# A projection tile's two moving pieces meet at a token that depends on the tile's index

## The chip, the cores and the metric

The kernel runs on one core of a Trainium2 chip. The metric is the device time of one execution in microseconds (us). Before the change three runs took 1004.9, 1005.52 and 1005.81 us; the median is 1005.52 us. A core has a matrix engine (TensorE, PE in the profile, with a loader for its weights, PEld), a vector engine (VectorE, DVE), a scalar engine (ScalarE, ACT), GpSimd (POOL) and a queue engine that issues most of the transfers (SyncE, SP). They run side by side and meet through semaphores.

## The reference: what is computed

The kernel is one layer of a hybrid sequence model over L = 528 tokens: 16 learned meta tokens and then 512 real ones, each 2048 wide. After a root-mean-square norm one input projection gives all the quantities of two branches; the branches' outputs are joined, go through an output projection and are added to the residual, and a last norm follows.

```python
hn = _rmsnorm(h_res, norm_in_g[l])
P = hn @ w_in[l]
Pr, Pc = P[..., :RW_COLS], P[..., RW_COLS:]
prev = jnp.pad(Pr[:, :-1], ((0, 0), (1, 0), (0, 0)))
Pr = Pr + (prev - Pr) * mu_shift[l]          # r, k, v, g of 1024 columns, and two of 64
...
y = _rwkv7_recurrence(...)                   # 16 heads of 64, in chunks of 64 tokens
y_a = (yn + bonus) * jax.nn.silu(g_r)
y_b = Bg * _causal_depthwise_conv(Cg * hc, conv_w[l]) * jax.nn.silu(g_c)
mix = jnp.concatenate([y_a, y_b], axis=-1)
h_res = h_res + mix @ w_out[l]
out = _rmsnorm(h_res, norm_f_g)[:, N_META:]
```

The first branch needs, for each token, the token before it (the shift by `mu_shift`), the second a convolution over three tokens. The meta tokens are dropped at the end, but k and v of the meta tokens enter the recurrence.

## The kernel before

**The projection.** The product `hn @ w_in` is made of 65 output tiles of 128 columns each: eight each of r, k, v and g of the first branch, one called lora (the two 64-wide parts), and eight each of B, C, h and gc of the second branch. The results stand with the 128 columns on the partitions and the tokens along the free axis. Input and weights are each split into a high and a low part in a rounded 32-bit format (`xh`, `xl`; `hi`, `lo` of a weight tile `w`), and three products make up the result: hi by xh, hi by xl, lo by xh. The contraction of 2048 runs in 16 blocks of 128 (`kt`). Each matmul instruction loads a 128 x 128 block of weights (the stationary operand, an LDWEIGHTS in the profile) and streams token columns past it (the moving operand); its result goes to a bank of PSUM that holds 512 such columns.

**The pieces.** Since 528 or 514 tokens don't go into one bank, the tokens are cut into two pieces, each with a PSUM tile of its own. There are three sets of ranges. `FULL` (k, v, lora) is tokens 0 to 256 and 256 to 528. `TAIL` (r, C, h, g) leaves out the meta tokens but for the last two, which shift and convolution need: 14 to 272 and 272 to 528. `REAL` (B, gc) is tokens 16 to 528 in one piece. The generator `steps` issues, for a quarter of the contraction (four blocks), first the twelve matmuls of the first piece and then the twelve of the second: 48 matmuls per piece and 96 per tile of two pieces. The piece's tokens are read from `xh` and `xl`, which have a row of 576 32-bit words per block.

**After the matmuls.** `scaled` multiplies each piece by the tokens' norm factor on DVE, from PSUM into one SBUF tile (`pr` or another); `shift_full` and `shift_real` add the shift, with one operation on ACT and one or two on DVE.

**What sets the order.** TensorE's order is written out by hand. `mains` is a generator that issues the projection's matmuls one by one, in the order of `plan`, and yields for each the time that it is reckoned to take, 0.43 ns a column. The rest of the program (`prepare` for a pair of heads, `invert`, the recurrence) issues its own matmuls and calls `fill(ns)` in between, which takes steps of `mains` until their reckoned times add up to that many ns; so projection matmuls fill the time in which the chain of the recurrence waits for other engines. `later(ns, ...)` puts off a transfer in the same reckoned time. The other engines' order is set by a scheduler from the order of issue and priorities; transfers on SP follow in that order too. Weights come ahead of use: three buffers for the raw halves of a tile (`wr`), six for split quarters (`w`); ACT makes the high part (L138), DVE or POOL the low one (L139).

The lines that matter: `FULL` and `TAIL` at L313 to L315, the matmul at L326 in `steps`, `main`, `scaled` (L345), `shift_full` and `shift_real`, the uses in `use`, and the loop at the end of `mains`. The first four tiles (lora, k, r, B, all of index 0) are issued by `mains` itself with the constant ranges. Recurrence lines named below: L451 sums for the norm factor, L674 products of a pair's chunks, L999 and L1003 the recurrence's chunk step, L1236 the output projection.

Of the kernel before, what the change touches and what calls it, by code (L numbers as in the profile page):

```python
# [23 lines left out]
L = SEQ + META  # L24
# [57 lines left out]
def hymba_kernel(ctx: ExitStack, tc: tile.TileContext, xt, xtok, front, w_in, w_out, pv, lup, cst, msk, gf, out):  # L82
# [33 lines left out]
    tile_of = {"r": 0, "k": 8, "v": 16, "g": 24, "lora": 32, "B": 33, "C": 41, "h": 49, "gc": 57}  # L116
    for what, i in plan:
        m = tile_of[what] + i
# [58 lines left out]
    def tm(name):  # L177
        return tp.tile([P, LP], F32, tag="tm", name=name, bufs=3)
# [134 lines left out]
    FULL = ((0, 256), (256, L))  # L313
    TAIL = ((14, 272), (272, L))
    REAL = ((META, L),)  # L315

    def steps(ps, ranges, k4, q, ks=range(4), rs_=range(2)):
        hi, lo = quarters[q]
# [12 lines left out]
    def banks(ranges, name, pool, tag):  # L331
        return [pool.tile([P, b - a], F32, tag=tag, name=f"ps_{name}_{r}") for r, (a, b) in enumerate(ranges)]

    def main(j, ranges, name):
        prefetch(2 * j + 4)
        ps = banks(ranges, name, pm, "main")
        for k4 in range(4):
            if k4 == 1:
                prefetch(2 * j + 5)
            yield from steps(ps, ranges, k4, 4 * j + k4)  # L340
        return ps

    def scaled(ranges, ps, dst, base):
        for (a, b), p in zip(ranges, ps):
            nc.vector.tensor_tensor(out=dst[:, a - base : b - base], in0=p, in1=rs[:, a:b], op=ALU.mult)  # L345

    def shift_full(ps, m, name, dst):
        pr = tp.tile([P, L + 1], F32, tag="pr", name=f"pr_{name}", bufs=2)
        nc.gpsimd.memset(pr[:, 0:1], 0.0)
        scaled(FULL, ps, pr, -1)  # L350
        sh = tm(f"sh_{name}")[:, 0:L]
        nc.scalar.activation(sh, pr[:, 0:L], AF.Copy, scale=col(V_MU, m))
        for (a, b), d in dst:
            nc.vector.scalar_tensor_tensor(
                out=d, in0=pr[:, a + 1 : b + 1], scalar=omm[:, m : m + 1], in1=sh[:, a:b], op0=ALU.mult, op1=ALU.add
            )

    def shift_real(ps, m, name, dst):
        pr = tp.tile([P, L + 1], F32, tag="pr", name=f"pr_{name}", bufs=2)
        scaled(TAIL, ps, pr, 14)  # L360
        sh = tm(f"sh_{name}")[:, 0:SEQ]
        nc.scalar.activation(sh, pr[:, 1 : SEQ + 1], AF.Copy, scale=col(V_MU, m))
        nc.vector.scalar_tensor_tensor(
            out=dst, in0=pr[:, 2 : SEQ + 2], scalar=omm[:, m : m + 1], in1=sh, op0=ALU.mult, op1=ALU.add
        )

    def padded(t):
        return (((0, META), t[:, 0:META]), ((META, L), t[:, CH:LP]))
# [5 lines left out]

    def use_lora(ps):
        pre = tm("lora_pre")[:, 0:L]
        shift_full(ps, 32, "lora", (((0, L), pre),))
        th = tr("lora_th")[0:64, 0:L]
        al = tr("lora_al")[0:64, 0:L]
        nc.scalar.activation(th, pre[0:64], AF.Tanh)  # L380
        nc.vector.tensor_copy(al, pre[64:128])
        for j, t in enumerate((th, al)):
            nc.scalar.copy(la[0:64, j], t)
            nc.vector.tensor_tensor(out=la[64:128, j], in0=t, in1=la[0:64, j].bitcast(F32), op=ALU.subtract)
# [6 lines left out]
    def use(what, i, ps):  # L391
        if what == "lora":
            use_lora(ps)
        elif what in ("k", "v"):
            t = cq.tile([P, LP], F32, tag=what, name=f"{what}{i}")
            nc.gpsimd.memset(t[:, META:CH], 0.0)
            shift_full(ps, tile_of[what] + i, f"{what}{i}", padded(t))
            got[what, i] = t
        elif what in ("r", "g"):
            t = cq.tile([P, SEQ], F32, tag=f"r{i % 2}" if what == "r" else "g", name=f"{what}{i}")  # L400
            shift_real(ps, tile_of[what] + i, f"{what}{i}", t)
            if what == "g":
                gate(t, f"r{i}")
                later(14000, lambda: nc.sync.dma_start(gated[i], t))
            got[what, i] = t
        elif what == "C":
            u = tm(f"u{i}")
            scaled(TAIL, ps, u, 14)
            got[what, i] = u
        elif what == "h":  # L410
            u = got["C", i]
            hh = tm(f"hh{i}")
            with behind_of("turned"):
                scaled(TAIL, ps, hh, 14)
            n = SEQ + 2
            nc.gpsimd.tensor_tensor(out=u[:, 0:n], in0=u[:, 0:n], in1=hh[:, 0:n], op=ALU.mult)
            cv = tp.tile([P, SEQ], F32, tag="cw", name=f"cv{i}")
            nc.scalar.activation(cv, u[:, 0:SEQ], AF.Copy, scale=col(V_CW, i))
            for j in (1, 2):
                with behind_of("conv"):  # L420
                    nc.vector.scalar_tensor_tensor(
                        out=cv, in0=u[:, j : j + SEQ], scalar=col(V_CW, 8 * j + i), in1=cv, op0=ALU.mult, op1=ALU.add
                    )
            got[what, i] = cv
            if i == 0:
                nc.gpsimd.tensor_tensor(out=cv, in0=cv, in1=got["B", 0], op=ALU.mult)
        elif what == "B":
            b = tm(f"b{i}")[:, 0:SEQ] if i else tp.tile([P, SEQ], F32, name="b0")
            scaled(REAL, ps, b, META)
            got[what, i] = b  # L430
            if i:
                nc.gpsimd.tensor_tensor(out=got["h", i], in0=got["h", i], in1=b, op=ALU.mult)
        else:
            cv = got["h", i]
            g = tm(f"gc{i}")[:, 0:SEQ]
            with behind_of("split"):
                scaled(REAL, ps, g, META)
            gate(g, f"c{i}")
            o = direct.get(8 + i, cv)
            nc.vector.scalar_tensor_tensor(out=o, in0=cv, scalar=0.5, in1=g, op0=ALU.mult, op1=ALU.mult)  # L440
            if o is cv:
                later(9000, lambda: nc.sync.dma_start(mixd[8 + i], cv))
        ready.add((what, i))
# [29 lines left out]
    def mains():  # L473
        pa = banks(FULL, "lora", pm, "main")
        pb = banks(FULL, "k0", pz, "tz")
        pc = banks(TAIL, "r0", pm, "main")
        pd = [pi.tile([P, SEQ], F32, tag="ser", name="ps_B0")]
        four = ((pa, FULL), (pb, FULL), (pc, TAIL), (pd, REAL))
        for k in range(4):
            for n, (ps, rg) in enumerate(four):  # L480
                if k == n == 0:
                    hi, lo = quarters[0]
                    for ww, xx, first in ((hi, xh, True), (lo, xh, False), (hi, xl, False)):
                        for p, (a, b) in zip(ps, rg):
                            nc.tensor.matmul(p, ww[:, 0:P], xx[:, 0, a:b], start=first, stop=False)
                            yield (b - a) * 0.43
                    continue
                yield from steps(ps, rg, 0, 2 * n, (k,))
        for k4 in range(1, 4):
            for n, (ps, rg) in enumerate(four):  # L490
                h = 4 * (k4 // 2) + n
                if k4 == 2:
                    prefetch(h + 3)
                if (k4, n) == (3, 3):
                    for ks, part in ((range(1), 0), (range(1, 3), 4), (range(3, 4), None)):
                        yield from steps(ps, rg, k4, 2 * h + k4 % 2, ks)
                        if part is not None:
                            token_scale(yb, part)
                        if part == 4:
                            use("lora", 0, pa)  # L500
                            use("k", 0, pb)
                    continue
                for r in range(2 if n < 3 else 1):
                    if (k4, n, r) == (3, 1, 1):
                        yb = token_scale_sums()
                    yield from steps(ps, rg, k4, 2 * h + k4 % 2, range(4), (r,))
        use("r", 0, pc)
        use("B", 0, pd)
        for j in range(4, len(plan)):
            what, i = plan[j]  # L510
            rg = FULL if what in ("k", "v") else REAL if what in ("B", "gc") else TAIL
            ps = yield from main(j, rg, f"{what}{i}")
            if (what, i) == ("h", 0):
                state["conv"] = low[4 * j + 6]
            if what == "gc" and i < 4:
                state["split"] = low[4 * j + 4]
            use(what, i, ps)
# [1001 lines left out]
```

## Time and profile before

| What | Value |
|---|---|
| Median of three runs | 1005.52 us (1004.9 to 1005.81) |
| Span of the profiled execution, first to last instruction | 1003.4 us |
| Granted TensorE clock over the span | 0.998 |
| TensorE busy | 992.7 us, 9,723 matmuls |
| Weight loads busy | 914.6 us |
| DVE, ACT, POOL busy | 681.1, 394.9, 272.1 us |
| Mean transfer rate | 174 GB/s |

The profile is of one execution; only its span is told, so the 2.1 us between it and the median are taken as what lies around the span. A row of a group names the line, engine, operation, the tile written and those read, shapes and the count, then the time that its instructions cover and the mean length of one. A row of the timeline has the start in us from the span's start and the time covered, then engine, line, operation, tiles, shapes and how many neighbours were merged. A row of the chain has start, length, engine, tile, line and count. A row of a window has its bounds, its length, TensorE's busy time with the count, the granted clock, the transfers' share and rate. Matmuls overlap, so their lengths add up to more than the time they take; the distance from one start to the next is what a stream of them costs.

### The profile page before, as it was taken

What the parts mean: (1) busy time and instruction counts of PE and PEld (TensorE: products, weight loads), DVE (VectorE), ACT (ScalarE), POOL (GpSimd) and SP (SyncE); (2) the same over time, 40 slices, a digit from 0 to 9 for tenths busy, and PEclk for the clock granted to TensorE, in tenths of its full rate; (3) what the DMA queues carried; (4) which work ended last, traced back from release to release, by engine and by line L of the source; (5) the groups of instructions that cost most, each with busy time, mean ns of one, the idle gap of its engine ahead of it and who ended that gap; (6) DMA issues with size and microseconds to landing.
All of it is one profiled execution on the core that took longest, in us unless ns stands there. A gap on an engine that the chain in (4) does not pass through costs nothing.

```text
span 1003.4 us, 23673 instructions
## 1 busy us (share of the span) xinstructions
PE 992.7 (99%) x9723; PEld 914.6 (91%) x9723; DVE 681.1 (68%) x1247; ACT 394.9 (39%) x729; POOL 272.1 (27%) x284
## 2 busy tenths in 40 slices
PE   9999999999999999999999999999999999999996
PEld 8999999999998999998999998989889898788885
DVE  6777866587765569655569654245554597997897
ACT  7553423344323434323434322223232435546453
POOL 0122524233232323232423223223332333001001
PEclk9999999999999999999999999999999999999999
DMA  9525485546665364864263855968674688797654
GB/s 322 153 90 148 122 222 147 163 122 148 162 167 170 102 166 94 221 163 119 85 171 98 219 148 162 324 204 247 201 228 93 178 267 211 187 299 191 159 127 168
DMA packets 185036, 174.82 MB, mean 174 GB/s; under 512 B 121568, under 2 KB 142816, under 8 KB 184416
## 3 DMA queue, kind: packets, MB, share of 16 engines
q1 hardware_dynamic: 182336, 164.40, 57.0%
q0 software_dynamic: 2304, 8.39, 4.9%
q8 instruction: 76, 1.25, 0.5%
q10 hardware_dynamic: 288, 0.52, 0.1%
q14 instruction: 32, 0.26, 0.1%
HBM read 136.92 MB, written 36.35 MB: 173 GB/s over the span
## 4 chain that ended last, share of the span: by engine, by line
PE 91%; DVE 5%; issue 1%; DMA 1%; ACT 0%; POOL 0%; DVEq 0%; SPq 0%; ACTq 0%; POOLq 0%
PE ps_h L326 9%; PE ps_k L326 9%; PE ps_v L326 9%; PE ps_g L326 9%; PE ps_C L326 9%; PE ps_r L326 9%; PE ps_B L326 9%; PE ps_gc L326 9%; PE M L1236 5%; PE P L1236 2%; PE g L674 2%; DVE o L1207 2%; PE Q L1236 1%; PE ps_lora L326 1%; PE zs L999 1%
## 5 line engine op out<-in xcount | busy, mean ns | idle before, releaser
L139 POOL TENSOR_TENSOR w<-wr,w 128x512 fp32r<-128x512 f32 x119 | 172.2, 1447 | 360.9 <-ACT w L138 305.1
L138 ACT CAST w<-wr 128x512 fp32r<-128x512 f32 x252 | 153.2, 618 | 289.0 <-PE ps_C L326 48.7
L139 DVE TENSOR_TENSOR w<-wr,w 128x512 fp32r<-128x512 f32 x133 | 98.5, 746 | 104.4 <-ACT w L138 104.0
L326 PE MATMUL ps_k<-xh,w 128*128 128x256 f32 (+1 forms) x512 | 96.1, 285 | 0.0
L326 PE MATMUL ps_r<-xh,w 128*128 128x258 f32 (+1 forms) x512 | 95.1, 281 | 0.0
L326 PE MATMUL ps_v<-xh,w 128*128 128x272 f32 (+1 forms) x512 | 94.9, 284 | 0.0
L326 PE MATMUL ps_h<-xh,w 128*128 128x256 f32 (+1 forms) x512 | 94.6, 283 | 0.0
L326 PE MATMUL ps_C<-xh,w 128*128 128x256 f32 (+1 forms) x512 | 93.2, 281 | 0.0
L326 PE MATMUL ps_g<-xh,w 128*128 128x256 f32 (+1 forms) x512 | 92.1, 281 | 0.0
L326 PE MATMUL ps_B<-xh,w 128*128 128x512 f32 x256 | 83.5, 395 | 0.0
L326 PE MATMUL ps_gc<-xh,w 128*128 128x512 f32 x256 | 81.6, 393 | 0.0
L326 PEld LDWEIGHTS ps_k<-xh,w 128*128 128x128 f32 x512 | 80.4, 190 | 0.5
L326 PEld LDWEIGHTS ps_h<-xh,w 128*128 128x128 f32 x512 | 79.6, 188 | 1.3 <-issue 0.6
L326 PEld LDWEIGHTS ps_r<-xh,w 128*128 128x128 f32 x512 | 80.1, 188 | 0.3
L326 PEld LDWEIGHTS ps_v<-xh,w 128*128 128x128 f32 x512 | 79.9, 189 | 0.3
L326 PEld LDWEIGHTS ps_C<-xh,w 128*128 128x128 f32 x512 | 79.2, 188 | 0.6
L326 PEld LDWEIGHTS ps_g<-xh,w 128*128 128x128 f32 x512 | 79.1, 189 | 0.3
L326 PE MATMUL ps_k<-xl,w 128*128 128x256 f32 (+1 forms) x256 | 72.8, 284 | 0.0
L326 PE MATMUL ps_v<-xl,w 128*128 128x256 f32 (+1 forms) x256 | 72.6, 284 | 0.0
L326 PE MATMUL ps_h<-xl,w 128*128 128x258 f32 (+1 forms) x256 | 71.9, 281 | 0.5 <-issue 0.5
L326 PE MATMUL ps_g<-xl,w 128*128 128x258 f32 (+1 forms) x256 | 72.3, 282 | 0.0
L326 PE MATMUL ps_r<-xl,w 128*128 128x258 f32 (+1 forms) x256 | 72.0, 281 | 0.0
(321 smaller groups left out, 2258.9 us busy)
## 6 DMA issues: line engine op xcount, KB each, us to landing
wr<-in_w_in_dram SPq DMA_DIRECT2D x126, 512.0 KB
ct<-opd SPq DMA_DIRECT2D x64, 288.0 KB
wo<-in_w_out_dram SPq DMA_DIRECT2D x24, 512.0 KB
x<-in_w_out_dram POOLq DMA_DIRECT2D x16, 512.0 KB, 6.0
opd<-ar SPq DMA_DIRECT2D x8, 576.0 KB
opd<-gt SPq DMA_DIRECT2D x16, 288.0 KB
opd<-bt SPq DMA_DIRECT2D x64, 64.0 KB
x<-in_w_out_dram SPq DMA_DIRECT2D x8, 512.0 KB
```

Of the source, the lines that this page charges most:

```text
L138: nc.scalar.copy(hi, rq)
L139: low[q] = eng.tensor_tensor(out=lo, in0=rq, in1=hi.bitcast(F32), op=ALU.subtract).ins
L326: nc.tensor.matmul(ps[r], ww[:, w], xx[:, kt, a:b], start=(kt == 0 and n == 0), stop=(kt == KT - 1 and n == 2))
L674: nc.tensor.matmul(z[h][:, c - c0], bk[hs, c, h : h + 2, :].rearrange("p a s -> p (a s)"), ar[hs, c].rearrange("p a s -> p (a s)"), start= ...
L999: nc.tensor.matmul(d[hs, j], w, x[hs], start=(a == 0), stop=(a == b - 1))
L1207: last = nc.vector.tensor_tensor(out=lo, in0=rq, in1=hi.bitcast(F32), op=ALU.subtract)
L1236: nc.tensor.matmul(bank[s], left(prod, jj, m, s), w, start=(jj == 0 and n == 0), stop=(jj == 7 and n == 2))
```

## The change

The border between the two pieces becomes a function of the tile's index i (0 to 7), the same for k and v, and the same for r, C, h and g. lora keeps the old border, B and gc their single piece.

```diff
     FULL = ((0, 256), (256, L))
     TAIL = ((14, 272), (272, L))
     REAL = ((META, L),)
+    FULL_AT = (256, 264, 272, 260, 288, 264, 258, 280)
+    TAIL_AT = (272, 270, 274, 276, 286, 270, 280, 272)
+
+    def pieces(what, i):
+        if what in ("B", "gc"):
+            return REAL
+        if what in ("k", "v"):
+            return (0, FULL_AT[i]), (FULL_AT[i], L)
+        return (14, TAIL_AT[i]), (TAIL_AT[i], L)
...
-    def shift_full(ps, m, name, dst):
+    def shift_full(ps, m, name, dst, rg):
...
-        scaled(FULL, ps, pr, -1)
+        scaled(rg, ps, pr, -1)
...
-    def shift_real(ps, m, name, dst):
+    def shift_real(ps, m, name, dst, rg):
...
-        scaled(TAIL, ps, pr, 14)
+        scaled(rg, ps, pr, 14)
...
-            scaled(TAIL, ps, u, 14)
+            scaled(pieces(what, i), ps, u, 14)
...
-            rg = FULL if what in ("k", "v") else REAL if what in ("B", "gc") else TAIL
-            ps = yield from main(j, rg, f"{what}{i}")
+            ps = yield from main(j, pieces(what, i), f"{what}{i}")
```

With L = 528 the pieces of index 0 to 7 have these columns, first and second: for k and v 256 and 272, 264 and 264, 272 and 256, 260 and 268, 288 and 240, 264 and 264, 258 and 270, 280 and 248; for r, C, h and g 258 and 256, 256 and 258, 260 and 254, 262 and 252, 272 and 242, 256 and 258, 266 and 248, 258 and 256.

More of the change, by code (lines that the diff above doesn't have):

```diff
@@ L376, in use_lora @@
         pre = tm("lora_pre")[:, 0:L]
-        shift_full(ps, 32, "lora", (((0, L), pre),))
+        shift_full(ps, 32, "lora", (((0, L), pre),), FULL)
         th = tr("lora_th")[0:64, 0:L]
@@ L396, in use @@
             nc.gpsimd.memset(t[:, META:CH], 0.0)
-            shift_full(ps, tile_of[what] + i, f"{what}{i}", padded(t))
+            shift_full(ps, tile_of[what] + i, f"{what}{i}", padded(t), pieces(what, i))
             got[what, i] = t
@@ L400, in use @@
             t = cq.tile([P, SEQ], F32, tag=f"r{i % 2}" if what == "r" else "g", name=f"{what}{i}")
-            shift_real(ps, tile_of[what] + i, f"{what}{i}", t)
+            shift_real(ps, tile_of[what] + i, f"{what}{i}", t, pieces(what, i))
             if what == "g":
@@ L413, in use @@
             with behind_of("turned"):
-                scaled(TAIL, ps, hh, 14)
+                scaled(pieces(what, i), ps, hh, 14)
             n = SEQ + 2
```

## The prediction

> **What bounds the kernel now.** I read the page's head and the clock row first, then the chain of waits, then two long windows, then the waits of the weight loader, and last the timeline inside single projection tiles.
>
> ```profile
> span 1003.4 us, 23673 instructions
> PE 992.7 (99%) x9723; PEld 914.6 (91%) x9723; DVE 681.1 (68%) x1247; ACT 394.9 (39%) x729; POOL 272.1 (27%) x284
> PEclk9999999999999999999999999999999999999999
> PE 91%; DVE 5%; issue 1%; DMA 1%; ACT 0%; POOL 0%; DVEq 0%; SPq 0%; ACTq 0%; POOLq 0%
> ```
> ```profile
> 55.00:605.00 550.00, 549.98 (x5219) 1.00 0.57 147
> 605.00:845.00 240.00, 239.53 (x3464) 1.00 0.72 216
> ```
> ```profile
> PEld ps_B L326 <- DVE w L139: 0.4, 1, 0.4
> ```
>
> TensorE is busy for 99% of the span at a full clock, and it makes up 91% of the chain that ended last. The windows leave it 0.02 us idle in 550 us and 0.47 us in the next 240 us. The only wait of a projection tile for split weights in the whole trace is 0.4 us. So between 55 and 845 us time is matmuls laid end to end, and what counts is how far apart two of them start. The listed duration of a matmul (some 280 ns) overlaps with its neighbours and is of no use for that.
>
> The start-to-start spacing can be read off the timeline: take two starts of the xl matmuls of one piece; between neighbouring xl matmuls lie three spacings.
>
> ```profile
> 469.83 0.28 PE L326 MATMUL ps_k<-xl,w 128*128 128x256 f32 x1
> ...
> 470.89 0.28 PE L326 MATMUL ps_k<-xl,w 128*128 128x256 f32 x1
> ...
> 471.25 0.28 PE L326 MATMUL ps_k<-xl,w 128*128 128x272 f32 x1
> ...
> 472.36 0.29 PE L326 MATMUL ps_k<-xl,w 128*128 128x272 f32 x1
> ```
> ```profile
> 132.26 0.28 PE L326 MATMUL ps_C<-xl,w 128*128 128x258 f32 x1
> ...
> 133.34 0.28 PE L326 MATMUL ps_C<-xl,w 128*128 128x258 f32 x1
> ...
> 133.69 0.28 PE L326 MATMUL ps_C<-xl,w 128*128 128x256 f32 x1
> ...
> 134.71 0.28 PE L326 MATMUL ps_C<-xl,w 128*128 128x256 f32 x1
> ```
> ```profile
> 620.71 0.28 PE L326 MATMUL ps_C<-xl,w 128*128 128x256 f32 x1
> ...
> 621.77 0.28 PE L326 MATMUL ps_C<-xl,w 128*128 128x256 f32 x1
> ```
> ```profile
> 132.30 11.20 PE ps_C L326 x96
> 469.87 11.57 PE ps_k L326 x96
> 532.78 11.54 PE ps_v L326 x96
> 619.32 11.38 PE ps_C L326 x96
> 819.75 10.90 PE ps_B L326 x48
> ```
>
> Each pair of rows spans nine spacings. A full tile (k): 1.06/9 = 117.8 ns at 256 columns from token 0, 1.11/9 = 123.3 ns at 272 columns from token 256. A tail tile (C): 1.08/9 = 120.0 ns at 258 columns from token 14, and 256 columns from token 272 take 113.3 ns in the first C tile and 117.8 ns in a later one. The same shape thus has two speeds, 4.5 ns apart, which is also the difference between the chain's 11.20 and 11.38 us for a C tile. A 512-column matmul takes 10.90/48 = 227.1 ns.
>
> **The change part by part.** It alters no product and no count: TensorE still issues 9,723 matmuls and as many weight loads. It moves the border between the two pieces in 38 tiles: k and v with index 1 to 7 (14 tiles), r, C, h and g with index 1 to 6 (24 tiles); each piece has 48 matmuls. Index 0, index 7 of the tail tiles, lora, and the one-piece tiles B and gc stay. Were time strictly in proportion to columns, the border would not matter, since a tile keeps its 528 or 514 columns. Three things can break that.
>
> First, pieces under 256 columns. The full tiles get 240 (index 4) and 248 (index 7), the tail tiles 254, 252, 242 and 248 (index 2, 3, 4, 6). That is 2 + 16 + 2 = 20 pieces, 960 matmuls. No row shows a matmul of this kind with fewer than 256 columns. What a matmul costs when there is almost nothing to stream is seen elsewhere:
>
> ```profile
> 45.10 0.81 PE L451 MATMUL pss<-cs,accd 128*128 128x1 f32 x6
> L451 PE MATMUL pss<-cs,accd 128*128 128x1 f32 x8 | 0.9, 240 | 0.0
> ```
> ```profile
> L999 PEld LDWEIGHTS zs<-ct 64*64 64x64 f32 x256 | 13.1, 136 | 0.0
> L326 PEld LDWEIGHTS ps_k<-xl,w 128*128 128x128 f32 x256 | 48.3, 189 | 0.2
> ```
>
> Six matmuls of one column, each with its own 128-column weights, take 0.81 us with the last one's 0.25 us: (0.81 - 0.25)/5 = 112 ns apart. They wait for their weights: a load of 64 columns lasts 136 ns and one of 128 lasts 189, so 53 ns per 64 columns, some 106 ns for 128. Every projection matmul has such a load too. So below 256 columns I expect a floor instead of a gain: at least 112 ns, at most the 117.8 ns of 256 columns. I take 115.5, the mean of the two speeds of the nearest row, 256 columns from token 272.
>
> On TensorE: Matmul & The Clock Gate of the Trainium skill (section Back-to-back issue gap) speaks against this floor with its isolated gap, N/2.4 + 2.5 ns, linear in N; by it a 240-column matmul would take an estimated 102.5 ns and every border would cost the same, so that the change would be worth nothing (first rival). The same page's LDWEIGHTS section gives P/1.2, 107 ns for 128 columns, and there the trace agrees (106 ns).
>
> Second, the wider partner. From 256 to 272 columns I interpolate 117.8 to 123.3 (0.344 ns a column), above that 123.3 to 227.1 at 512 (0.43 ns a column): 280 columns 126.8, 288 columns 130.2.
>
> Third, where a piece begins. On that line 258 columns would be 118.5 ns; the tail's first piece, which begins at token 14 (byte 56, off a multiple of 16), takes 120.0. I charge 1.5 ns for every piece that begins at a token not a multiple of 4: the new borders 258, 270, 274 and 286. From below this may be nothing (the two extra columns explain it).
>
> Now each pair against today's. Full tiles, 117.8 + 123.3 = 241.1 ns; indices 1 to 7: 264+264 0.0; 272+256 (115.5 at an even border) -2.3; 260+268 0.0; 288+240 130.2 + 115.5 = +4.6; 264+264 0.0; 258+270 +1.5; 280+248 +1.2. Sum +5.0 ns, x 48 x 2 kinds = +0.5 us. Tail tiles, 120.0 + 115.5 = 235.5 ns; indices 1 to 6: 256+258, both off, 119.3 + 120.0 = +3.8; 260+254 +2.2; 262+252 +1.4; 272+242 124.8 + 117.0 = +6.3; 256+258 +3.8; 266+248 +2.7. Sum +20.2 ns, x 48 x 4 kinds = +3.9 us. All of it is on the path, since TensorE has no idle time there: +4.4 us.
>
> With a floor of 112, no charge for the start and the quick speed for the 256 columns at border 272 the same sums give -0.5 - 1.7 = -2.2 us; with a floor of 117.8 and the charge, +1.1 + 5.6 = +6.8 us.
>
> What is costed at nothing: the evacuations on DVE.
>
> ```profile
> L345 DVE TENSOR_TENSOR pr_k<-ps_k,rs 128x256 f32<-128x256 f32 (+1 forms) x16 | 6.5, 420 | 3.8 <-PE ps_k L326 3.8
> ACT w L138 <- PE ps_C L326: 48.7, 25, 5.0
> ```
>
> Two of 420 ns per tile become two of other widths with the same columns together; a tile's matmuls go on in other banks for over 11 us meanwhile. Were that cover gone, a first piece of 288 columns would hold back its successor by the extra 32/256 x 420 = 53 ns. The changed steps (0.43 ns a column in the generator) also shift where the recurrence's matmuls and the timed DMAs fall in: in the built programs TensorE's order differs at 74 places, mostly one matmul earlier or later. ACT, DVE, POOL and SP swap a few neighbours; on SP the load of the tile numbered wr24 goes ahead of nine queued items, one being the store of ar of pair 1. ACT's splits mostly wait for TensorE to free a buffer (48.7 us behind ps_C alone), so the weights are ahead of their use and I cost the swaps at nothing, with the 0.4 us above as all that could be won.
>
> The profiled execution shows a span of 1003.4 us; the three timed runs have a median of 1005.52, 2.1 us more for what lies around the span. The sum is made on the span and carried over: 1005.5 + 4.4 = 1009.9 us. From no change, a measurement of this kernel can tell about 0.2%, here 2 us.
>
> **The rivals.** (1) Borders are free: narrow pieces gain what wide ones lose, the start costs nothing; 1005.5 us, or anything within 2 us, as when the floor is 112 and only some of the starts cost. For it: from 256 to 512 columns time grows nearly in proportion. Against it: the 112 ns for one column.
>
> (2) Faster: a new border puts the matmuls into the quicker of their two speeds. The place is every changed tile, the price 4.5 ns a matmul, as between the two C tiles. If one of both pieces of all 38 tiles went over, that is 38 x 48 x 4.5 ns = 8.2 us less; against the +4.4 it decides once half of them do, and with all 1005.5 + 4.4 - 8.2 = 1001.7 us. For it: the speed is a matter of circumstance, since equal shapes differ. Against it: the first tail piece, off its multiple, lies above the line at 120.0, and new borders add such starts.
>
> (3) Narrow pieces lose the fast rate of this number format altogether. Unrounded fp32 shows what that would be:
>
> ```profile
> 80.03 1.99 PE g L674 x32
> L674 PE MATMUL g<-ar,bk 64*128 64x128 f32 x288 | 20.4, 283 | 0.0
> ```
>
> Here 288 instructions make 144 products (8 pairs, 9 chunks, 2 heads), two heads on separate halves of the array, so 32 of them are 8 chunks: 249 ns per 128 columns, 1.94 ns a column against 0.46 for k. At 246 columns that is 478 instead of 115.5 ns: 960 x 0.362 = 348 us, 1353 us. For it: no piece here is under 256. Against it: the built matmuls of 240 and 256 columns are instructions of the same form.
>
> (4) A swapped split or load leaves TensorE waiting: one POOL split late (1.45 us by its group) at two places adds 2.9 us, 1012.8 us. For it: the 0.4 us shows little margin at one spot. Against it: nothing else waits.
>
> ```profile
> L139 POOL TENSOR_TENSOR w<-wr,w 128x512 fp32r<-128x512 f32 x119 | 172.2, 1447 | 360.9 <-ACT w L138 305.1
> ```
>
> **How the numbers follow.** Forecast (floor and starts) 0.58, rival 1 0.16, rival 2 0.14, rival 3 0.07, rival 4 0.05. Slower: 0.58 + 0.07 + 0.05 = 0.70; same 0.16; faster 0.14. The range runs from the sum's lower bound, 1005.5 - 2.2 = 1003.3, to its upper, 1005.5 + 6.8 = 1012.3, rounded up to 1013 for rival 4; outside are rival 3 and about 0.10 of rival 2. The forecast's own range is 1007.6 to 1012.3.
>
> **What would show it.** In the changed kernel's timeline: pieces of 240 to 254 columns start 112 to 118 ns apart, not 106; 288 columns near 130; 256 columns from token 14 near 119. The chain's row for a C tile of index 4 should be near 11.6 us instead of 11.2, and TensorE still without idle time to 845 us. Wrong it is if the narrow pieces follow at under 110 ns or far above 120, if the two speeds redistribute by several ns across whole tiles, or if a wait for w appears on the weight loader.

## The result, and the profile after

The changed kernel takes 1020.95 us (median of four runs, 1020.77 to 1021.77), the kernel before beside it 1005.21 us (1003.84 to 1005.81). The ratio is 1.016, with a 95% interval of 1.0145 to 1.0174: slower by 15.7 us, where 4.4 were forecast. 1020.95 us lies above the range, which ended at 1013.0.

The page of the changed kernel, its head, its clock row and the shares of the chain that ended last:

```profile
span 1019.0 us, 23673 instructions
PE 1002.3 (98%) x9723; PEld 923.9 (91%) x9723; DVE 678.8 (67%) x1247; ACT 394.9 (39%) x729; POOL 262.7 (26%) x284
PEclk9999999999999999999998999999999999999999
PE 91%; DVE 5%; DMA 2%; issue 1%; ACT 0%; SPq 0%; DVEq 0%; POOL 0%; ACTq 0%
```

The span grew by 15.6 us (1003.4 to 1019.0), and the granted clock over it fell from 0.998 to 0.993, with the same counts of instructions on every engine. These rows look almost like those of before. Only the 8 in the clock row, and 2% of DMA in a chain that had 1%, hint at something. The two long windows of the prediction say more (window, its length, TensorE busy, loader, DVE, ACT, POOL, granted clock, transfers):

```profile
55.00:605.00 550.00, 543.62 (x5020) 524.39 (x5019) 360.33 (x731) 197.41 (x364) 162.80 (x179) 0.99 0.56 145
605.00:845.00 240.00, 239.84 (x3590) 214.06 (x3589) 127.94 (x208) 69.91 (x132) 72.09 (x58) 1.00 0.68 205
```

TensorE, idle for 0.02 us between 55 and 605 us before, is now idle for 6.38 us, and the clock is not full. The waits of TensorE (tile, who ended the wait, us in total, times, longest) have two rows that the kernel before has not:

```profile
PE ta L572 <- ACT tz L577: 4.4, 1, 4.4
PE ps_h L335 <- DVE pr_g L354: 2.0, 1, 2.0
```

Two single waits, 1.97 and 4.41 us, are the whole idle time. The timeline of TensorE shows them, with the last matmul ahead of each (the wait stands in brackets); the last two rows show the pace behind the second:

```profile
284.54 0.28 PE L335 MATMUL ps_h<-xh,w 128*128 128x256 f32 x1
286.79 0.39 PE L335 MATMUL ps_h<-xh,w 128*128 128x258 f32 x1 [1.97 <-DVE pr_g L354]
...
533.77 0.28 PE L335 MATMUL ps_r<-xh,w 128*128 128x258 f32 x1
538.46 0.59 PE L572 MATMUL ta<-la,luh 128*128 128x272 f32 x1 [4.41 <-ACT tz L577]
...
539.08 0.42 PE L335 MATMUL ps_r<-xh,w 128*128 128x258 f32 x1
539.29 0.42 PE L335 MATMUL ps_r<-xl,w 128*128 128x258 f32 x1
```

**The first place** is the second piece of the h tile of index 1. It waits for a PSUM bank, and the bank is held by the g tile of index 3, whose piece DVE has not yet evacuated (multiplied out of PSUM by `scaled`, which frees the bank). DVE's timeline around it, after the change:

```profile
275.20 0.17 DVE L757 TENSOR_SCALAR nd<-nd 72x16 f32<-72x16 f32 x1 [6.97 <-DMA nd<-sn]
...
280.14 0.42 DVE L354 TENSOR_TENSOR pr_g<-ps_g,rs 128x262 f32<-128x262 f32 x1
...
285.39 1.01 DVE L775 TENSOR_TENSOR prod<-d,y 72x512 f32<-72x512 f32 x1
286.32 0.41 DVE L354 TENSOR_TENSOR pr_g<-ps_g,rs 128x252 f32<-128x252 f32 x1
```

and before, for the same two evacuations:

```profile
270.00 0.43 DVE L345 TENSOR_TENSOR pr_g<-ps_g,rs 128x258 f32<-128x258 f32 x1
271.38 0.43 DVE L345 TENSOR_TENSOR pr_g<-ps_g,rs 128x256 f32<-128x256 f32 x1 [0.95 <-PE ps_g L326]
271.72 0.16 DVE L749 TENSOR_SCALAR nd<-nd 72x16 f32<-72x16 f32 x1
```

The rows on 72 partitions (`nd`, `y`, `tt`, `prod`) are the inversion of a pair's blocks (`invert`, here of pair 3), a chain of short dependent operations on DVE. Before, both evacuations stood ahead of it, and the second ran as soon as TensorE had finished the piece. Now they stand behind 7 and 30 of its operations. DVE takes its queue in order: it sits idle for 6.97 us, to 275.20 us, for a transfer that `nd` needs, although TensorE started the last matmul of g3 at 271.60, and then works through the chain. The second evacuation starts 15 us later than before, and TensorE goes on 0.06 us after its end.

The transfer is late because SP's order has changed as well. First after the change, then before:

```profile
263.48 0.33 SPq L146 DMA_DIRECT2D wr<-in_w_in_dram  x1
...
273.73 0.32 SPq L622 DMA_DIRECT2D nd<-sn  x1
```
```profile
267.33 0.33 SPq L614 DMA_DIRECT2D nd<-sn  x1
```

SP sends off the transfer of `nd` 6.4 us later than before. Two weight loads now stand ahead of it, at 263.48 and 267.31, where the second of them came behind it before (267.76), and the store `sn` that it reads goes off at 269.58 instead of 264.54. So the first place is a matter of two queues too, SP's and DVE's.

**The second place** has one link more. DVE and then ACT, after the change:

```profile
532.85 0.44 DVE L354 TENSOR_TENSOR pr_k<-ps_k,rs 128x280 f32<-128x280 f32 x1
...
536.70 0.40 DVE L354 TENSOR_TENSOR pr_k<-ps_k,rs 128x248 f32<-128x248 f32 x1
```
```profile
537.14 0.74 ACT L361 ACTIVATE sh_k<-pr_k,pvt 128x528 f32<-128x528 f32 x1 [8.87 <-DVE pr_k L354]
537.78 0.26 ACT L576 ACTIVATE tz<-tz,hv 128x16 f32<-128x16 f32 x1
537.94 0.47 ACT L577 ACTIVATE tz<-tz,hv 128x256 f32<-128x256 f32 x1
```

and before:

```profile
519.26 0.36 DVE L345 TENSOR_TENSOR pr_k<-ps_k,rs 128x256 f32<-128x256 f32 x1
...
520.53 0.44 DVE L345 TENSOR_TENSOR pr_k<-ps_k,rs 128x272 f32<-128x272 f32 x1 [0.82 <-PE ps_k L326]
```

The evacuations of k7 stand behind 29 and 33 operations of the inversion of pair 6 (before: 2 and 3). ACT's shift `sh_k` needs both; ACT is idle for 8.87 us for it. Behind it in ACT's queue is the tanh that empties the PSUM buffer `tz`, and TensorE's next low-rank product `ta` (L572) needs that buffer. TensorE itself has matmuls of r7 to issue, but `ta` stands ahead of them in its queue.

**The clock.** Behind each wait TensorE ran at half its clock:

```profile
288.00:291.40 3.40, 3.40 (x19) 3.40 (x18) 3.05 (x5) 2.20 (x5) 0.47 (x1) 0.52 0.45 124
537.30:544.10 6.80, 5.64 (x26) 5.64 (x27) 3.75 (x5) 3.51 (x9) 2.15 (x3) 0.50 0.01 2
```

The clock's own record has these stretches as 3.413 us from 288.17 and 6.827 us from 537.34; the kernel before has none between its first microseconds and its last five. Matmuls at half clock follow at 0.21 us (539.08 to 539.29 above) instead of about 0.12, so 45% of the time is lost: 0.45 x 3.41 = 1.5 us, and 0.45 x (544.17 - 538.46) = 2.6 us of the part after the wait. The bill is 1.97 + 4.41 + 1.5 + 2.6 = 10.5 us for two late evacuations, and the remaining 15.6 - 10.5 = 5.1 us are for the pieces themselves.

**The pieces.** The same kind of rows as in the prediction (xl matmuls of one piece; nine spacings between the two rows), first C of index 4, then k of index 4:

```profile
637.15 0.29 PE L335 MATMUL ps_C<-xl,w 128*128 128x272 f32 x1
...
638.29 0.29 PE L335 MATMUL ps_C<-xl,w 128*128 128x272 f32 x1
638.66 0.28 PE L335 MATMUL ps_C<-xl,w 128*128 128x242 f32 x1
...
639.69 0.28 PE L335 MATMUL ps_C<-xl,w 128*128 128x242 f32 x1
```
```profile
327.74 0.29 PE L335 MATMUL ps_k<-xl,w 128*128 128x288 f32 x1
...
328.94 0.30 PE L335 MATMUL ps_k<-xl,w 128*128 128x288 f32 x1
329.32 0.27 PE L335 MATMUL ps_k<-xl,w 128*128 128x240 f32 x1
...
330.32 0.27 PE L335 MATMUL ps_k<-xl,w 128*128 128x240 f32 x1
```

272 columns from token 14 take 1.14/9 = 126.7 ns, 242 columns 1.03/9 = 114.4, 288 columns 1.20/9 = 133.3, 240 columns 1.00/9 = 111.1. The start-to-start means within all pieces of a kind, worked out from the starts in the two traces:

| Columns, first token | before, ns | after, ns | put in the prediction |
|---|---|---|---|
| 240, 242 | | 111.7, 112.9 | 115.5, 117.0 |
| 248 (full; tail), 252, 254 | | 114.7; 115.7, 117.1, 118.1 | 115.5, 115.5, 117.0 |
| 256 from 0; from 272, tail; from 272, full | 117.3; 115.7; - | 117.5; 116.2; 119.7 | 117.8; 115.5; 115.5 |
| 256 from 14; 258 from 270 | | 119.9; 119.7 | 119.3; 120.0 |
| 258, 260, 264 from 0 | | 120.9, 119.8, 122.8 | 118.5, 119.2, 120.6 |
| 272, 280, 288 from 0 | | 124.7, 128.6, 132.9 | 123.3, 126.8, 130.2 |
| 264 from 264; 268 from 260; 270 from 258 | | 120.7; 123.3; 125.0 | 120.6; 121.9; 124.1 |
| 260, 262, 266 from 14 | | 121.0, 120.5, 124.0 | 120.7, 121.4, 122.7 |
| 272 from 14; 272 from 256 | -; 123.6 | 127.0; 123.8 | 124.8; 123.3 |
| 512 from 16 | 227.9 | 227.9 | 227.1 |

With these means a full tile's pair (240.9 ns before) grows over indices 1 to 7 2.6, 3.4, 2.2, 3.7, 2.6, 5.0 and 2.4 = 21.9 ns, times 96 = 2.1 us; a tail tile's pair (235.9 before) over indices 1 to 6 3.7, 3.2, 1.7, 4.0, 3.7 and 3.8 = 20.1 ns, times 192 = 3.9 us. Together 6.0 us, against the 5.1 that the waits leave; the two reckonings differ by 0.9 us.

The tokens at which a piece begins do not decide its speed alone. In the changed kernel 256 columns from token 272 follow at 116.2 ns in the tail tiles and at 119.7 in k and v of index 2. And the second piece of C of index 0, whose border did not move, went from 113.4 ns to 117.9, that of g of index 0 from 117.6 to 114.6. Over all tiles whose pieces are as before such changes come to some 0.1 us; what sets them is not shown.

### The profile page after: what moved, and what is told of

Read it like the earlier page. It is cut to its first block, busy times and chain, and to the rows that moved or that the text cites. A ratio compares the mean times of both kernels' runs of the same rounds, so it can differ in the third digit from the quotient of the medians.

```text
span 1019.0 us, 23673 instructions
## 1 busy us (share of the span) xinstructions
PE 1002.3 (98%) x9723; PEld 923.9 (91%) x9723; DVE 678.8 (67%) x1247; ACT 394.9 (39%) x729; POOL 262.7 (26%) x284
## 4 chain that ended last, share of the span: by engine, by line
PE 91%; DVE 5%; DMA 2%; issue 1%; ACT 0%; SPq 0%; DVEq 0%; POOL 0%; ACTq 0%
PE ps_h L335 9%; PE ps_v L335 9%; PE ps_g L335 9%; PE ps_gc L335 9%; PE ps_B L335 9%; PE ps_r L335 9%; PE ps_k L335 8%; PE ps_C L335 8%; PE M L1244 5%; PE P L1244 3%; PE g L682 2%; PE Q L1244 2%; DVE o L1215 1%; PE zs L1007 1%; PE ps_lora L335 1%; PE zy L1011 1%
## 5 line engine op out<-in xcount | busy, mean ns | idle before, releaser
L335 PE MATMUL ps_h<-xh,w 128*128 128x258 f32 (+9 forms) x512 | 96.9, 286 | 2.1 <-DVE pr_g L354 2.0
L335 PE MATMUL ps_r<-xh,w 128*128 128x258 f32 (+9 forms) x512 | 97.3, 286 | 0.0
L335 PE MATMUL ps_k<-xh,w 128*128 128x264 f32 (+10 forms) x512 | 97.2, 286 | 0.0
L335 PE MATMUL ps_v<-xh,w 128*128 128x264 f32 (+10 forms) x512 | 96.4, 285 | 0.0
L335 PE MATMUL ps_C<-xh,w 128*128 128x258 f32 (+9 forms) x512 | 94.6, 283 | 0.0
L335 PE MATMUL ps_g<-xh,w 128*128 128x258 f32 (+9 forms) x512 | 93.0, 282 | 0.0
L335 PE MATMUL ps_r<-xl,w 128*128 128x258 f32 (+9 forms) x256 | 73.2, 286 | 0.0
L335 PE MATMUL ps_h<-xl,w 128*128 128x258 f32 (+9 forms) x256 | 73.1, 286 | 0.0
L335 PE MATMUL ps_k<-xl,w 128*128 128x264 f32 (+10 forms) x256 | 72.8, 284 | 0.0
L335 PE MATMUL ps_v<-xl,w 128*128 128x264 f32 (+10 forms) x256 | 72.8, 284 | 0.0
```

The costliest lines, as they stand in the source:

```text
L335: nc.tensor.matmul(ps[r], ww[:, w], xx[:, kt, a:b], start=(kt == 0 and n == 0), stop=(kt == KT - 1 and n == 2))
```

## The experiments

The theory from here on: moving two of the borders (index 3 of the tail tiles, index 7 of k and v) makes the scheduler put the evacuations of g3 and k7 behind an inversion in DVE's queue; this alone costs some 11 us, and the widths and starts of the pieces some 5 to 6. The rivals: the new order of TensorE's own matmuls (74 places) costs it; or it is all the pieces' speed, the narrow ones' above all. Edits are against the changed kernel where FULL_AT or TAIL_AT occur, else against the kernel before.

**Two borders back.**

```diff
-    FULL_AT = (256, 264, 272, 260, 288, 264, 258, 280)
-    TAIL_AT = (272, 270, 274, 276, 286, 270, 280, 272)
+    FULL_AT = (256, 264, 272, 260, 288, 264, 258, 264)
+    TAIL_AT = (272, 270, 274, 272, 286, 270, 280, 272)
```

> The changed kernel with two entries put back to borders that leave no piece under 256 columns: k and v of index 7 at 264 instead of 280, r, C, h and g of index 3 at 272 instead of 276. In the built program the evacuations of g3 and k7 on DVE then stand ahead of the block inversion again, while TensorE's order differs from before at the same 74 places. Theory A (DVE's order makes TensorE wait for PSUM, and each wait is followed by a stretch at half clock): no wait of TensorE over 0.5 us between 55 and 845 us, clock 0.998, time = widths alone, 1009.5 us (1008 to 1011). Rival B (TensorE's own shifted order makes the waits): they stay, 1019 to 1021 us. Rival C (the moving pieces themselves lower the clock): half-clock stretches stay, above 1013 us.

1010.13 us, ratio 1.0049 (1.0034 to 1.0064). In the windows of this run TensorE has no idle time again, at a full clock:

```profile
55.00:605.00 550.00, 550.00 (x5196) 529.66 (x5196) 364.24 (x741) 200.33 (x370) 171.13 (x181) 1.00 0.57 147
```

Both waits are gone with two of the 13 moved indices altered, and with them 10.8 of the 15.7 us (1020.95 - 1010.13). Index 3 of the tail tiles is back at 272, which by the table saves 1.7 ns x 192 = 0.3 us; index 7 of k and v is at 264 and not at the old 256, which saves nothing (2.6 ns a pair against 2.4). That leaves 10.5 for the waits and the clock. TensorE's 74 changed places are all still there, so they are not what costs. What is left is +4.9 us against the 1005.21 above, or +5.2 against the 1004.97 beside this run; by the table it should be 5.7.

**The order alone, on DVE.** The kernel before, no border moved; only the four evacuations are held behind operations of the inversion: k7's behind 29 and 33, as in the changed kernel, g3's behind 3 and 29, where the changed kernel has 7 and 30. `held[i]` is a list of some of the operations of pair i's inversion, in order.

```diff
-    def scaled(ranges, ps, dst, base):
-        for (a, b), p in zip(ranges, ps):
-            nc.vector.tensor_tensor(out=dst[:, a - base : b - base], in0=p, in1=rs[:, a:b], op=ALU.mult)
+    def scaled(ranges, ps, dst, base, behind=()):
+        for n, ((a, b), p) in enumerate(zip(ranges, ps)):
+            with tc.issue_after(behind[n]) if behind else nullcontext():
+                nc.vector.tensor_tensor(out=dst[:, a - base : b - base], in0=p, in1=rs[:, a:b], op=ALU.mult)
...
-        scaled(FULL, ps, pr, -1)
+        scaled(FULL, ps, pr, -1, (held[6][8], held[6][9]) if name == "k7" else ())
...
-        scaled(TAIL, ps, pr, 14)
+        scaled(TAIL, ps, pr, 14, (held[3][2], held[3][8]) if name == "g3" else ())
```

> The kernel before with all its borders, TensorE's order identical; only the two evacuations of g3 are held behind 3 and 29 operations of pair 3's block inversion on DVE, and those of k7 behind 29 and 33 of pair 6's. Theory A: TensorE waits once for pr_g's and once for pr_k's evacuation (2 and 4.4 us), the clock is halved for 3.4 and 6.8 us, +11 us, 1016.5 us (1013 to 1018). Rivals B and C: none of the borders has moved, so 1005.5 us.

1005.05 us, ratio 1.0002 (0.9993 to 1.0011), and no wait: a miss. The late evacuation is there, and later than in the kernel before by 12 us, but ACT's queue (the second fence) has the tanh of `tz` ahead of the shift:

```profile
532.93 0.43 DVE L346 TENSOR_TENSOR pr_k<-ps_k,rs 128x272 f32<-128x272 f32 x1
```
```profile
521.69 0.47 ACT L571 ACTIVATE tz<-tz,hv 128x256 f32<-128x256 f32 x1
...
533.39 0.74 ACT L353 ACTIVATE sh_k<-pr_k,pvt 128x528 f32<-128x528 f32 x1 [2.40 <-DVE pr_k L346]
```

With the hold the scheduler put the tanh ahead of the shift. At g3 the inversion of pair 3 was not itself late here: SP's order is that of before, `nd` is there without a wait, and the second evacuation starts at 281.87 us instead of 286.32. So an evacuation late on DVE cost nothing by itself in this run; there must be something behind it in a second queue, or the chain ahead of it must stand still.

**The order alone, on two queues.** The kernel before with k7's two evacuations held as above (g3 left alone), and the tanh held behind the shift, as in the changed kernel.

```diff
-            with tc.high_priority(offset=AHEAD):
+            with tc.issue_after(state["sh_k7"]) if name == "tz7" else tc.high_priority(offset=AHEAD):
```

> All borders as before and TensorE's order identical to before. k7's two evacuations stand behind 29 and 33 operations of pair 6's inversion on DVE, as in the changed kernel, and on ACT the tanh of tz7 stands behind the shift of k7, as there too (in the run with the order alone the scheduler had moved the tanh ahead of it). Theory A, refined (the late evacuation reaches TensorE through ACT's queue, which works in order: the shift waits for DVE, the tanh behind it holds the PSUM buffer that the ta matmul needs): a wait of some 4 us before ta, then 6.8 us at half clock, 1012 us (1010 to 1014). If a border under 256 columns is needed for the loss: 1005 us.

1013.54 us, ratio 1.0083 (1.0068 to 1.0098). TensorE's waits and ACT's timeline have the rows of the changed kernel, and the clock's record has 6.827 us at half:

```profile
PE ta L566 <- ACT tz L571: 5.8, 1, 5.8
```
```profile
531.23 0.73 ACT L353 ACTIVATE sh_k<-pr_k,pvt 128x528 f32<-128x528 f32 x1 [4.15 <-DVE pr_k L346]
531.87 0.25 ACT L570 ACTIVATE tz<-tz,hv 128x16 f32<-128x16 f32 x1
```

No piece has another width or start here. The wait of 5.8 us and the half clock behind it, 0.45 x (538.28 - 532.54) = 2.6 us, make 8.4. So the order of the queues alone, without any border, makes 8.3 us (beside the two that were held, POOL's and SP's orders differ in the trace at 5 and 9 places). The like was not tried for g3, whose cause rests on the trace and on the runs with one border.

**One border each, at 274.** First k and v of index 7 alone (FULL_AT ends in 274, all else as before), then index 3 of r, C, h and g alone.

```diff
+    FULL_AT = (256, 256, 256, 256, 256, 256, 256, 274)
+    TAIL_AT = (272, 272, 272, 272, 272, 272, 272, 272)
```

> All borders as before but that of k and v of index 7: 274, so pieces of 274 and 254 columns. TensorE's order is identical to before; DVE's differs at 20 places, with k7's evacuations behind 30 and 33 operations of the inversion. By matmul width alone 2 x 48 x some 1 ns, +0.1 us: 1005.6 us (rival C). Theory A: the wait of the ta matmul for ACT's tz (4.4 us) and the half-clock stretch (3.4 to 6.8 us), +7.2 us: 1012.7 us (1009 to 1014).

1012.03 us, ratio 1.0067 (1.0052 to 1.0082). The row of the waits is that of the changed kernel, and 6.827 us are at half clock:

```profile
PE ta L572 <- ACT tz L577: 4.4, 1, 4.4
```

TensorE's order is the same in the built program as before the change, so it is not its order that does it.

```diff
+    FULL_AT = (256, 256, 256, 256, 256, 256, 256, 256)
+    TAIL_AT = (272, 272, 272, 274, 272, 272, 272, 272)
```

> Only r, C, h and g of index 3 get a new border, 274, so 260 and 254 columns. In the built program g3's evacuations stand behind 18 and 33 operations of pair 3's inversion on DVE, TensorE's order differs at 14 places. Widths alone: 4 tiles x 48 x 3.5 ns = +0.7 us, 1005.7 us. Theory A: the second piece of h1 waits some 2 us for g3's evacuation, and 3.4 us at half clock follow: +3.9 us more, 1009.6 us (1008 to 1011).

1012.95 us (1012.05 to 1014.88), ratio 1.0084 (1.0067 to 1.0101), and 3.413 us at half clock:

```profile
PE ps_h L335 <- DVE pr_g L354: 3.9, 1, 3.9
```

The place and the releaser are as expected, the size is not: the wait is twice as long as in the changed kernel. The second evacuation stands behind 33 operations here instead of 30, and the last three end 2.5 us after the thirtieth. By the spacings of its own trace the pieces cost 1.0 us: 0.8 for the moved tiles, and 0.2 for the second piece of C of index 1, whose border did not move and which went from 113.4 to 118.0 ns. So 3.9 + 1.5 (half clock) + 1.0 = 6.4 us; the profiled execution, at 1012.05 us the quickest of the four, shows a span of 1010.0 us, 6.6 over that of before. The median is 7.5 over that of the runs beside it. The two longer executions (1013.65 and 1014.88 us) have a granted clock of 0.994 instead of 0.995 and 0.996, which would fit a second stretch at half clock; no trace of them shows it.

**One border at 272.** The same as the first of these two, with 272 for 274: k and v of index 7 have 272 and 256 columns instead of 274 and 254.

```diff
+    FULL_AT = (256, 256, 256, 256, 256, 256, 256, 272)
+    TAIL_AT = (272, 272, 272, 272, 272, 272, 272, 272)
```

> Only k and v of index 7 get a new border, 272, so 272 and 256 columns: two tokens from the run with 274. The built program's order is the same as before on every engine. By the changed kernel's spacings for 272 and 256 (124.6 and 119.6 against 117.7 and 123.5 ns) 96 x 3 ns = +0.3 us, no wait: 1005.3 us (1004.5 to 1006). If moving this border costs by itself what 274 costs: 1012 us.

1005.29 us (ten runs, 1004.66 to 1006.0), ratio 1.0001 (0.9991 to 1.001), no wait. In its trace DVE, ACT, POOL and SP have the order of before in every place; at 274, where one piece has fewer than 256 columns, k7's evacuations stand behind 30 and 33 operations of the inversion. For index 3 of the tail tiles g3's evacuations stand ahead of the inversion at 270 (in the next run) and behind it at 274. Two tokens are thus worth 6.7 us (1012.03 - 1005.29), and between 272 and 274 it is a step and not a slope. The scheduler appears to reckon a matmul of fewer than 256 columns much dearer than one of 256, and so expects g3 and k7 to be ready late; that reckoning itself was not read out, only its step in the built order.

**No piece under 256 columns, every border moved.** This keeps the starts off a multiple and the wide first pieces, and takes the narrow ones away.

```diff
+    FULL_AT = (256, 264, 272, 260, 264, 264, 258, 264)
+    TAIL_AT = (272, 270, 270, 270, 270, 270, 270, 272)
```

> Borders moved in the same 38 tiles, but none leaves a piece under 256 columns: k and v 256, 264, 272, 260, 264, 264, 258, 264; r, C, h and g 270 for index 1 to 6. By the spacings of the changed kernel's own trace (256 at token 14 and 258 at token 270 each 120 ns, 264 pairs 243, 272+256 244, 258+270 246): +1.6 and +5.0 us, 1011.8 us (1010 to 1013), no wait, full clock. By the prediction's own numbers (264 pairs 0, -2.3, +1.5; tails +3.8): +4.3 us, 1009.8 us. If the narrow pieces were what costs: 1005.5 us.

1011.26 us, ratio 1.006 (1.0043 to 1.0077), no wait. Without a single narrow piece the pieces cost +6.3 us against the 1004.97 beside it, no less than the +5.2 with 14 of them in the run with two borders back. The narrow pieces are not what makes the 5 us.

**Very narrow pieces** (one run).

```diff
+    FULL_AT = (256, 400, 464, 496, 288, 264, 258, 264)
+    TAIL_AT = (272, 272, 272, 272, 272, 272, 272, 272)
```

> Only k and v move: index 1 to 3 get 400+128, 464+64 and 496+32 columns, index 4 to 7 288+240, 264+264, 258+270, 264+264; the other tiles as before. If a weight load sets a floor (112 ns, from the one-column matmuls): pieces of 128, 64 and 32 columns all follow each other at 112 ns, the pairs cost 291, 318 and 332 ns against 241, and with the other four (+1.2 us) the time is 1005 + 4.8 + 7.4 + 8.7 + 1.2 = 1027 us. If time goes on in proportion below 240 columns (0.45 ns a column): 61, 33 and 18 ns and 1006 us. If narrow pieces lost the format's fast rate (1.94 ns a column): 248 ns at 128 columns.

1027.31 us, against 1004.21 beside it. Pieces of 128 columns and of 32 (k of index 1 and 3):

```profile
78.74 0.28 PE L335 MATMUL ps_k<-xl,w 128*128 128x128 f32 x1
...
79.74 0.27 PE L335 MATMUL ps_k<-xl,w 128*128 128x128 f32 x1
```
```profile
220.40 0.26 PE L335 MATMUL ps_k<-xl,w 128*128 128x32 f32 x1
...
221.41 0.26 PE L335 MATMUL ps_k<-xl,w 128*128 128x32 f32 x1
```

1.00/9 = 111.1 ns and 1.01/9 = 112.2 ns: a quarter of the columns saves nothing. Here is the floor of 112 ns that the prediction took from matmuls of one column. Only the second matmul of each twelve follows sooner, at some 57 ns with 128 columns and some 27 with 32. The Trainium skill's linear gap (TensorE: Matmul & The Clock Gate, section Back-to-back issue gap), from which the prediction took its counter-estimate, would by estimate give 32/2.4 + 2.5 = 15.8 ns. The section of the Trainium skill states it for an isolated matmul and says that it counts too little at few columns, for want of the weight load. The measurement agrees with this limit: in a stream where each matmul has its own weights the linear gap does not hold.

**The rows of the input moved.** The kernel before, its program and order unchanged, but with the rows of `xh` and `xl` beginning 2, 4, 8 or 16 words later (8, 16, 32 and 64 bytes). The first has several runs, the others one each.

```diff
-    xh = xp.tile([P, KT, LX], F32R, name="xh")
-    xl = xp.tile([P, KT, LX], F32R, name="xl")
+    xh = xp.tile([P, KT, LX], F32R, name="xh")[:, :, 2:LX]
+    xl = xp.tile([P, KT, LX], F32R, name="xl")[:, :, 2:LX]
```

> All borders as before, program order the same; every row of the two moving tensors begins 8 bytes later, so the tail's first piece begins on a multiple of 16 bytes and the other pieces begin 8 bytes off one. If being off costs 1.5 ns a matmul (the prediction's charge): tail first piece 118.5 instead of 120.1 ns, tail second piece +1.5, both full pieces +1.5, the 512-column pieces +1.5: (17 tiles x 3.0 + 16 x 1.5) x 48 ns = +3.6 us, 1008.6 us. If the start does not matter: 1005 us, and the 258-column piece stays at 120 ns.

1020.4 us, ratio 1.0152 (1.0137 to 1.0167), with TensorE at a full clock and no new wait beyond 0.6 us; it should have been 1008.6. From the chain:

```profile
478.41 11.82 PE ps_k L326 x96
...
834.48 11.20 PE ps_B L326 x48
```

A B tile takes 11.20 us instead of 10.90, a k tile 11.82 instead of 11.57. In means: 512 columns 233.3 ns (227.9 before), 256 from token 0 120.0 (117.3), 272 columns 126.6 (123.6), 256 from token 272 120.1 (115.7). And the tail's first piece, which by this move begins on a multiple of 32 bytes, stays at 120.3 (120.2).

> As the run with rows moved by 8 bytes, but by 16: the three starts that were on a multiple of 16 bytes stay on one (but leave their multiple of 32), the tail's first piece stays off. If 16 bytes is the line that counts: 512 columns at 227.9 ns, 1005 us. If 32 or 64 is: 512 columns at 233 ns, 256 at 120, 1018 to 1020 us.

1015.72 us, against 1004.21; 512 columns at 231.6 ns, 256 from token 0 at 118.6.

> Rows moved by 32 bytes: every start keeps its place within 32 bytes. If 16 or 32 bytes is the line that counts: spacings as before, 1005 us. If it is 64: 512 columns at 233 ns, 1018 to 1020 us. If the absolute place against the weights counts, something between.

1015.64 us, against 1004.21; 233.2 and 118.5 ns.

> The kernel before with the rows of both halves of the input beginning 16 words (64 bytes) later, program and order unchanged. Moves of 8, 16 and 32 bytes gave 1020.4, 1015.72 and 1015.64 us against 1005. If only the place within 64 bytes counts, this one is back at 1005 (within 2 us), 512 columns at 228 ns, 256 from token 0 at 117.5 ns. If it is a longer period, or any move costs because the rows then stand otherwise to the weights, it stays at 1012 or more, with 512 columns at 231 to 233 ns.

1013.1 us, against 1004.89; 229.3 and 118.9 ns. The B tile in the chain of this last run:

```profile
827.46 11.00 PE ps_B L326 x48
```

No move returns to 1005. So the place where the streamed rows begin is worth several ns a matmul; it is not a matter of a multiple of 16, 32 or 64 bytes alone, and what it is remains open: a longer period, or the rows' place against that of the weights or the output, would both do. The charge of 1.5 ns at a multiple of 4 tokens has the right sign for the tail tiles and the wrong rule.

## Why the prediction was wrong

By its own steps:

- **The evacuations and the other queues, costed at nothing: this step failed.** "ACT, DVE, POOL and SP swap a few neighbours ... I cost the swaps at nothing" named the splits of weights as the work that could come late, and their lead as the cover. What came late was the evacuation of PSUM, on which the prediction had only asked what a longer first piece costs (53 ns). It did not count past how many operations an evacuation was moved: 30 for g3, 33 for k7. A swap on SP, of the kind that the prediction noted at another load, made the first of these worse: DVE stood idle for 6.97 us for a transfer that SP sent off 6.4 us later. The counts were to be seen in the built order. The two late evacuations cost 10.5 us by the trace, and as much by putting the two borders back.
- **The half clock behind a wait** was in no step: 4.1 of the 10.5 us. Where the prediction priced a wait (rival 4, 1.45 us for a late split) it took its length alone.
- **Rival 4** was the right kind, a swap that leaves TensorE waiting at two places, at a chance of 0.05. Its place was wrong (no split was late by more than 0.4 us: the loader waits for `w` twice, 0.4 us each, where it waited 0.4 and 0.2 before), and its price, 2.9 us, was little over a quarter of the 10.5.
- **The widths and starts, +4.4 us: the sum nearly held, its parts less.** Measured +4.9 to 5.2 in the run with two borders back, 5.1 to 6.0 in the changed kernel. The tail's +3.9 is 3.9 by the spacings, partly by luck: index 4, put at +6.3 ns, came to 4.0, and indices 2, 3 and 6 came 0.3 to 1.1 ns dearer than put. The full tiles' +0.5 is 2.1: the wider first pieces follow 0.48 ns a column (117.5 at 256, 132.9 at 288) instead of 0.344 and 0.43, and at index 2 the 256 columns behind the wider piece follow at 119.7 instead of 115.5, which turns its -2.3 ns into +3.4.
- **The floor** is there at 112 ns, as the lower bound had it, but it is reached only at 240 columns; 248 to 254 columns follow the line from 256. Taking 115.5 for all of them was 4 ns too much at 240 and 242 and 1 to 2 too little at 252 and 254. The theory that the floor makes the change dear fell with the run that has no narrow piece and costs no less.
- **Rivals 1 to 3.** The borders were not free in the sum. None of the 38 moved tiles was faster as a whole. No narrow piece lost the fast rate (111.7 to 118.1 ns, not 478).
- **The signs set out beforehand.** Narrow pieces at 112 to 118 ns: yes. 288 columns near 130: 133. 256 from token 14 near 119: 119.9. The C tile of index 4 near 11.6 us: 11.54, as the chain has it below. TensorE without idle time: no, and that was the sign of the failure. The wait expected in that case was one for `w`, which did not come beyond 0.4 us. Of the signs of being wrong another came, the two speeds that change over a whole piece (C and g of index 0 above), but it was worth some 0.1 us in the tiles whose borders stayed.

```profile
634.31 11.54 PE ps_C L335 x96
```

## What to carry to other kernels

When a scheduler sets the order of the other engines, a change of a tile's size is also a change of their queues: compare the built order and count, for every operation that frees a buffer of the critical engine, how many operations it now stands behind and whether any of them waits for a transfer that is itself sent off later; follow it through the next in-order queue too. Price a wait of TensorE by its length plus the stretch at half clock that can follow (here 1.5 us on top of 1.97, and 2.6 on top of 4.41 and of 5.8). A column count at which a reckoning has a step (here 256) is worth trying from both sides: two tokens made 6.7 us.

## What was not expected of the hardware

- The clock falls after short waits. Waits of 1.97 and 3.9 us were each followed by one stretch of 3.413 us at half clock, waits of 4.4 (twice) and 5.8 us by one of 6.827 us. In the changed kernel one stretch begins when TensorE has work again (288.17, with work from 286.79), the other when it has none yet (537.34, with work from 538.46); over the four traces with such waits it begins 3.1 to 5.0 us after the start of the last matmul ahead of the wait. The end of the first stretch (291.58) and the start of the second (537.34) lie 72 x 3.413 us apart. This agrees with the free-running window of 3,413 ns of the Trainium skill (TensorE: Matmul & The Clock Gate, section What's actually happening). The advice of the same page of the Trainium skill to avoid gaps of more than some 3 us (section Why this matters for your kernels) is too generous here, since 1.97 us were enough.
- The idle part of such a window, and not the length of the wait alone, goes with the fall and with its length. With windows of 3.413 us laid back and forth from the start of each trace's half clock, the window ahead of the fall was idle for some 2.0 and 3.3 us (the changed kernel), 2.8 (274 for k and v), 3.4 (274 for the tail) and 3.4 (two queues); the window before that in the run with two queues was idle for 1.3 us, and the clock stayed full. The first window at half clock was idle for 0 and 0.6 us where the clock came back after it, and for 1.1, 1.1 and 1.6 where a second one followed.
- In a stream with 128 columns of weights per matmul, 32, 64 and 128 columns follow at 111 to 112 ns (but for the second of each twelve), 240 columns still at 111.7, and only above that does a column cost time.
- Moving the streamed rows by 8 bytes cost 15.3 us on a kernel of 1005 us with no other difference (512 columns 227.9 to 233.3 ns), and no move tried was free. The kernel before stands on a good place by this measure, and the reason is open.
